# One encoder layer with attention and Hyena: folded taps in tiles of their own, part of the Hyena projection's splitting and stores on GpSimd, and the last attention unit's sums on VectorE

## The chip, the cores and the metric

The kernel runs on one NeuronCore of a Trainium2 chip. The metric is device time in microseconds (us), and lower is better. A core has five engines that each work through an instruction queue in order: TensorE (PE, with weight loads shown apart as PEld), VectorE (DVE), ScalarE (ACT), GpSimd (POOL) and SyncE (SP). In this kernel SP only issues DMA transfers; GpSimd and ScalarE can issue them too. Matmuls write to PSUM banks, and everything else lies in SBUF or HBM.

## What is computed

One layer of an encoder over 2048 tokens of width 1024, in float32. One projection gives queries, keys and values of a grouped-query attention (8 query heads, 2 key heads of 64) and the 1536 columns `u` of a Hyena operator:

```python
a = rms_norm(h, norm1_g[i])
proj = a @ w_in[i]
q, k, v, u = jnp.split(proj, [Q_WIDTH, Q_WIDTH + KV_WIDTH, Q_WIDTH + 2 * KV_WIDTH], axis=-1)
...
att = block_attention(q, k, v)
hy = hyena_mixer(u, hy_conv_w[i], hy_conv_b[i], filt_w1[i], ..., filt_deltas[i], hy_skip_d[i])
mix = jnp.concatenate([rms_norm(att, attn_out_g[i]), rms_norm(hy, hy_out_g[i])], axis=-1)
h = h + mix @ w_out[i]
m = rms_norm(h, norm2_g[i])
h = h + jnp.square(jax.nn.relu(m @ w_mlp_in[i])) @ w_mlp_out[i]
```

The Hyena operator first runs a convolution of width 3 over `u`. It then multiplies in the frequency domain by filters that a small network makes, with a decay, and divides them by the sum of their absolute values:

```python
h = h @ w4                                                   # hidden (2048 x 64) times w4 (64 x 2048)
h = h * jnp.exp(-t * jnp.abs(deltas)[None, :])
taps = jnp.concatenate([fwd, zeros, bwd[:0:-1]], axis=0)
taps = taps / jnp.sum(jnp.abs(taps), axis=0, keepdims=True)
return jnp.fft.rfft(taps, axis=0)
```

## The kernel before

**Precision.** A float32 product is made of three faster ones: each operand is split into a high part (a rounded copy, made by ScalarE) and a low part (the rest, made by VectorE), and TensorE adds high x low, low x high and high x high (L160 to L162).

**Stages.** (1) `qkv_proj` makes q, k and v, and runs the filter network's hidden layers beside it. Its order on each engine is the order of the code. (2) `attention`, from about 234 to 1193 us. (3) Transforms of the filters and the long convolutions, the mixing projection and the MLP, to the end at 3089.4 us. The change touches the end of the first stage and the second.

**u_proj** (L417 to L511) is a generator that the other stages pump, one step at a time. It makes `u` for four blocks of 512 tokens, and for each of them 12 column blocks of 128 columns; n counts both. In the first pass over the columns the weights are made as well. `load_raw` fetches a raw block of w_in (512 KB) on SP's queue. `split(n)` scales it into `uws`, eight slices each: ScalarE's high part (L448), VectorE's low part (L449), then one store of both parts to `uw_d` (1 MB, L452) for the later passes. Block n then takes 24 matmuls into the PSUM tile `uo`. ScalarE copies that to `u` (L497), which frees the bank, and makes the middle tap of the width-3 convolution, `uy` (L505). VectorE adds the two outer taps (L509), and a store on SP's queue writes `u_d` (256 KB, L511). While block n is multiplied, split(n + 1) runs. Two buffers (`uw12`) alternate, so split(n + 1) writes the buffer of block n - 1 and must wait until its matmuls are done and its store has landed. Raw blocks 1 and 2 are loaded ahead; for n from 1 to 9 the loop loads raw block n + 2 into one of two buffers (`ring`).

When `qkv_proj` has ended, 28 more steps of u_proj are pumped (START), which brings blocks up to n = 4 back to back; the rest runs beside attention.

**attention** (L541 on) has 32 units (2 key heads by 16 tiles of 128 tokens, 4 heads at once) of 16 steps. In this stage a scheduler sets the order of instructions on each engine. Some 22 steps ahead of its use, `peak` multiplies keys and queries (`sc`, L558) and VectorE takes the maximum (`top`, L561). `weights` multiplies again in higher precision (`st`, L578 and L579), ScalarE takes the exponential into a tile `p` (L581; a ring of PB = 14), and GpSimd adds the p of 16 steps: `sum` (L586), and at the last step its two halves into two tiles `os` (L591). `weighted` multiplies p by the values (`o`, L599); after a unit's last step ScalarE copies o's halves into `os` (L602), GpSimd adds both tiles (`ob`, L604), and `finish` turns the result with four matmuls (`of`, L610) and divides.

**Side work of attention.** Beside each step it pumps a mix: the first step of `taps_ahead`, 24 steps of u_proj, and then both in turns. `taps_ahead` (L1376 on) loads w4 in four pieces on GpSimd's queue (L1382), splits them (`w4h` on ScalarE, L1385, and w4l on VectorE), and makes 64 pieces of the taps of 128 channels by 512 positions. For each: an exponential of the decay on ScalarE (`ex`, L1403), two matmuls (`ft`, L1406), a product on VectorE (`taps`, L1408), the sum and the difference with the reversed taps on VectorE, written over `ex` (L1413, L1414), a store of these (`taps_d`, 256 KB, L1417, SP's queue), and on ScalarE the absolute values of the taps with their sum (L1418), written over `taps`. So a `taps` tile is read by both folds before L1418 may write it. `ex` tiles are a ring of three, `taps` tiles a ring of two; the w4 pieces lie in the same rings before.

Of the kernel before, what the change touches and what calls it, by code (L numbers as in the profile page):

```python
# [20 lines left out]
P = 128  # L21
# [16 lines left out]
def f32(ap):  # L38
    return ap.bitcast(F32)
# [386 lines left out]
def u_proj(k):  # L426
# [17 lines left out]
    def split(n, raw):  # L444

        w = uws[n and 2 - n % 2]
        for d in range(ND):
            nc.scalar.mul(out=w[:, 0, d], in_=raw[:, d], mul=k.g1[:, d:d + 1])  # L448
            nc.vector.scalar_tensor_tensor(out=w[:, 1, d], in0=raw[:, d], scalar=k.g1[:, d:d + 1],  # L449
                                           in1=f32(w[:, 0, d]), op0=ALU.mult, op1=ALU.subtract)  # L450
            yield
        nc.sync.dma_start(out=k.uw_d[n], in_=f32(w))  # L452
        yield
# [7 lines left out]
    uws += [pair[:, 0], pair[:, 1]]  # L461
    for n in (1, 2):
        raws[n] = load_raw(n, k.pa.tile([P, ND, P], F32, name="uraw", tag="xs", bufs=3)[:])
    yield
    for _ in split(1, raws[1]):
        yield
    k.up = sbuf(k, "up")
    pu = k.up.__enter__()
    edge = pu.tile([P, nct, 2], F32, name="edge", bufs=1)
    for n in range(NB * nct):  # L470
        b, ct = NB - 1 - n // nct, n % nct
        w = uws[n and 2 - n % 2]
        if n == 1:
            ring = k.uf.tile([P, 2, ND, P], F32, name="uraw", tag="U")
        if 0 < n < nct - 2:
            raws[n + 2] = load_raw(n + 2, ring[:, n % 2])
        parts = iter(())
# [30 lines left out]
        for tap in (0, 2):  # L508
            nc.vector.scalar_tensor_tensor(out=y[:, :m], in0=u[:, tap:tap + m], scalar=cw[:, tap, ct:ct + 1],  # L509
                                           in1=y[:, :m], op0=ALU.mult, op1=ALU.add)  # L510
        nc.sync.dma_start(out=k.u_d[ct * P:(ct + 1) * P, t0:t0 + m], in_=y[:, :m])  # L511

# [29 lines left out]
def attention(k, a1, ps, side):  # L542
# [6 lines left out]
    nc.vector.memset(fold[HD:, HD:], 1.0)  # L549
    one = a1.tile([P, P], F32, name="one", bufs=1)  # L550
    nc.vector.memset(one[:], 1.0)
    ones = a1.tile([P, P], F32R, name="ones", bufs=1)
    nc.vector.tensor_copy(out=ones[:], in_=one[:])

# [19 lines left out]
    def weights(u, j):  # L574
        s = ps.get("st", "st")
        b, c = j // 4, slice(j % 4 * P, (j % 4 + 1) * P)
        hi, lo = kt[u.kv, b]
        nc.tensor.matmul(s[:], lo[:, c], u.q2[:].rearrange("p h t -> p (h t)"), start=True, stop=False)  # L578
        nc.tensor.matmul(s[:], hi[:, c], u.q[:].rearrange("p h t -> p (h t)"), start=False, stop=True)  # L579
        p = a1.tile([P, 512], F32, name="p", bufs=PB)  # L580
        nc.scalar.activation(out=p[:], in_=s[:], func=AF.Exp)  # L581
        if j == 0:
            u.p0 = p
            u.sum = a1.tile([P, 512], F32, name="sum", bufs=2)
        elif j < 15:
            nc.gpsimd.tensor_add(out=u.sum[:], in0=u.p0[:] if j == 1 else u.sum[:], in1=p[:])  # L586
        else:
            u.os = [a1.tile([P, 512], F32, name="os", bufs=OSB) for i in range(2)]
            for i in range(2):
                rows = slice(i * HD, (i + 1) * HD)  # L590
                nc.gpsimd.tensor_add(out=u.os[i][HD:], in0=u.sum[rows], in1=p[rows])  # L591
        return u, j, p

    def weighted(u, j, p):
# [5 lines left out]
        if j == 15:  # L600
            for i in range(2):
                nc.scalar.copy(out=u.os[i][:HD], in_=u.o[i * HD:(i + 1) * HD])  # L602
            u.both = a1.tile([P, 512], F32, name="ob", bufs=1)
            nc.gpsimd.tensor_add(out=u.both[:], in0=u.os[0][:], in1=u.os[1][:])  # L604

# [62 lines left out]
SH = 2  # L668
PB = 14
RATE = 0.95  # L670
# [4 lines left out]
OSB = 2  # L675
UW_VEC = 0, 1, 2, 3, 4, 5, 6, 7

# [697 lines left out]
def filter_taps(k, f1, ps):  # L1375
    nc, a = k.nc, k.a  # L1376
    w4h = f1.tile([P, 4, HYW], F32R, name="w4h")
    w4l = f1.tile([P, 4, HYW], F32R, name="w4l")
    w4s = [f1.tile([P, HYW], F32, name="w4", tag=t, bufs=b) for t, b in (("ex", 3),) * 3 + (("taps", 2),)]
    for c, w4 in enumerate(w4s):  # L1380
# [12 lines left out]
    for b in range(4):  # L1393
        s = slice(b * 512, (b + 1) * 512)
        for i in range(2):
            tr = f1.tile([P, 512], F32, name="tr", bufs=2)
            nc.sync.dma_start(out=tr[:], in_=a["trow"][i:i + 1, s].to_broadcast([P, 512]))
            for o in range(2):
                for ct in range(4):
                    ci = o * 8 + i * 4 + ct  # L1400
                    cs = slice(ct * P, (ct + 1) * P)
                    ex = f1.tile([P, 512], F32, name="ex", bufs=3)
                    nc.scalar.activation(out=ex[:], in_=tr[:], func=AF.Exp, scale=dn[:, ci:ci + 1])  # L1403
# [5 lines left out]
                    if i == 1 and b == 0:  # L1409
                        nc.vector.memset(tp[:, 0:1], 0.0)  # L1410
                    x, e = (t[:].rearrange("p (s m) -> p s m", m=P) for t in (tp, ex))
                    back = x[:, :, ::-1][:, :, :HF]
                    nc.vector.tensor_add(out=e[:, :, :HF], in0=x[:, :, :HF], in1=back)  # L1413
                    nc.vector.tensor_sub(out=e[:, :, HF:], in0=x[:, :, :HF], in1=back)  # L1414
                    if i == 0 and b == 0:
                        nc.vector.tensor_copy(out=first[:, o, :, ct], in_=ex[:, 0:HF + 1:HF])
                    nc.sync.dma_start(out=k.taps_d[o, cs, i * SEQ + b * 512:i * SEQ + (b + 1) * 512], in_=ex[:])  # L1417
                    nc.scalar.activation(out=tp[:], in_=tp[:], func=AF.Abs,  # L1418
                                         accum_out=ab[:, o, ct, 4 * i + b:4 * i + b + 1])
# [447 lines left out]
def encoder_layer(tc, a):  # L1867
    with ExitStack() as ctx:
        k = setup(tc, ctx, a)
        with sbuf(k, "hid") as hid, sbuf(k, "early") as k.early:  # L1870
            k.hc = hid.tile([P, 2, SEQ], F32R, name="hc")
            with sbuf(k, "uf") as k.uf:
# [6 lines left out]
                with sbuf(k, "at") as at:  # L1879
                    with Banks(k, "ps2", {"st": 2, "sc": 3, "o": 1, "u": 2}) as k.ps:  # L1880
                        taps = taps_ahead(k, k.ps)
                        attention(k, at, k.ps, chain(islice(taps, 1), islice(k.u, UFIRST), mixed(taps, MA, k.u, MB)))
                k.up.__exit__(None, None, None)
        with sbuf(k, "wa") as k.wa:
# [36 lines left out]
```

## Time and profile before

| | us |
|---|---|
| median of 3 runs | 3090.89 |
| lowest, highest | 3089.37, 3095.59 |
| the profiled execution, its own time | 3091.2 |
| its span (first to last instruction) | 3089.4 |
| TensorE busy | 2968.5 (96%) |
| VectorE busy | 2082.4 (67%) |
| GpSimd busy | 1647.9 (53%) |
| ScalarE busy | 1388.5 (45%) |

The mean granted clock of TensorE is 0.985 of full speed. A row of a timeline has the start and the duration in us, then engine, line, operation, what is written and read, shape and count; in brackets stands the engine's idle time just ahead and what ended it. A row of a group has the count, the busy time in us and the mean of one in ns behind the shape. A row of the waits has the waiting engine, tile and line, what it waited for, the sum in us, how often, and the longest. A row of the chain has start and duration, then engine or DMA, tile and line. "SPq" is SP's queue; its durations there are those of the issue, not of the transfer. A row of windows gives for each engine the busy time and the count of instructions.

### The profile page before, as it was taken

How to read it: one execution, taken by the hardware profiler on the slowest of the kernel's cores; microseconds unless marked ns; L12 is line 12 of the kernel's file. 1: busy time of each engine (PE TensorE's matmuls, PEld its weight loads, DVE VectorE, ACT ScalarE, POOL GpSimd, SP SyncE). 2: the span in 40 equal slices, each digit the busy share in tenths (PEclk: the TensorE clock that was granted, in tenths of full speed). 3: DMA queues.
4: the chain of work that ended last, by engine and by line, in shares of the span. 5: the costliest groups of instructions: out<-in, count | busy, mean ns of one | idle time of the engine just before them, and what ended most of it. 6: DMA issues, size and time to landing. Idle time of an engine off the chain costs nothing.

```text
span 3089.4 us, 40268 instructions
## 1 busy us (share of the span) xinstructions
PE 2968.5 (96%) x13386; PEld 2237.0 (72%) x13386; DVE 2082.4 (67%) x3153; ACT 1388.5 (45%) x2593; POOL 1647.9 (53%) x1336
## 2 busy tenths in 40 slices
PE   7998999999999998999999889999999899999998
PEld 6785666666666666765758767887888688888887
DVE  6778887777777764667475568778877554454455
ACT  6765555555555545543435553334333233223333
POOL 4333787877778773015555128777877462250010
PEclk9998999999999999999999999999999999999999
DMA  8766433243342245875746875445544492433454
GB/s 248 217 192 208 143 115 108 95 156 104 104 150 102 96 131 170 287 254 189 215 137 198 288 266 164 154 150 204 181 157 153 152 355 99 142 108 130 150 184 150
DMA packets 452769, 525.74 MB, mean 170 GB/s; under 512 B 30443, under 2 KB 316769, under 8 KB 445521
## 3 DMA queue, kind: packets, MB, share of 16 engines
q1 hardware_dynamic: 442656, 502.44, 49.9%
q0 software_dynamic: 5856, 16.23, 1.6%
q10 hardware_dynamic: 4048, 4.49, 0.4%
q8 instruction: 107, 1.75, 0.2%
q14 instruction: 102, 0.83, 0.1%
HBM read 321.72 MB, written 193.99 MB: 167 GB/s over the span
## 4 chain that ended last, share of the span: by engine, by line
PE 78%; DVE 5%; issue 4%; POOL 3%; ACT 2%; DMA 2%; SPq 0%; ACTq 0%; POOLq 0%; DVEq 0%
PE o L599 7%; PE y L160 7%; PE y L161 7%; PE y L162 7%; PE g L161 6%; PE g L162 5%; PE g L160 5%; PE X L1543 4%; PE st L578 4%; PE sc L558 3%; PE st L579 3%; PE uo L162 2%; PE uo L161 2%; PE uo L160 2%; PE b L1678 2%
## 5 line engine op out<-in xcount | busy, mean ns | idle before, releaser
L586 POOL TENSOR_TENSOR sum<-sum,p 128x512 f32<-128x512 f32 x416 | 554.4, 1333 | 115.0 <-ACT p L581 89.6
L561 DVE TENSOR_REDUCE top<-sc 128x1 f32<-128x512 f32 x512 | 345.1, 685 | 172.4 <-PE sc L558 169.8
L581 ACT ACTIVATE p<-st 128x512 f32<-128x512 f32 x512 | 299.8, 596 | 227.5 <-PE st L579 215.5
L160 PE MATMUL g<-mh,wop 128*128 128x512 f32 x896 | 350.9, 392 | 6.8 <-ACT wop L1009 6.8
L161 PE MATMUL g<-ml,wop 128*128 128x512 f32 x896 | 351.0, 392 | 3.5 <-DVE ml L1020 3.5
L162 PE MATMUL g<-mh,wop 128*128 128x512 f32 x896 | 351.0, 392 | 1.9 <-DVE wop L1010 1.9
L160 PE MATMUL y<-bh,ah 128*128 128x512 f32 x768 | 299.7, 390 | 12.7 <-ACT ah L1214 12.7
L1193 DVE TENSOR_TENSOR ah<-ar,ah 128x1024 fp32r<-128x1024 f32 x111 | 150.0, 1352 | 223.9 <-ACT ah L1192 221.5
L161 PE MATMUL y<-bh,ah 128*128 128x512 f32 x768 | 299.5, 390 | 0.0
L162 PE MATMUL y<-bh,ah 128*128 128x512 f32 x768 | 299.4, 390 | 0.0
L1192 ACT CAST ah<-ar 128x1024 fp32r<-128x1024 f32 x111 | 117.0, 1054 | 337.9 <-PE y L162 329.7
L599 PE MATMUL o<-p,vt 128*64 128x512 f32 x1024 | 241.9, 604 | 0.0
L578 PE MATMUL st<-q,kt 128*128 128x512 f32 x512 | 213.9, 418 | 8.8 <-ACT p L581 8.6
L558 PE MATMUL sc<-kt,q 128*128 128x512 f32 x512 | 204.2, 402 | 16.9 <-DVE top L561 10.5
L579 PE MATMUL st<-q,kt 128*128 128x512 f32 x512 | 201.2, 393 | 0.0
L160 PEld LDWEIGHTS g<-mh,wop 128*128 128x128 f32 x896 | 169.6, 189 | 42.9 <-ACT wop L1009 7.5
L161 PEld LDWEIGHTS g<-ml,wop 128*128 128x128 f32 x896 | 169.3, 189 | 39.8 <-DVE ml L1020 4.5
L162 PEld LDWEIGHTS g<-mh,wop 128*128 128x128 f32 x896 | 169.3, 189 | 38.2 <-DVE wop L1010 3.1
L1009 ACT CAST wop<-ws 128x512 fp32r<-128x512 f32 x128 | 79.3, 621 | 229.1 <-PE g L162 177.4
L160 PEld LDWEIGHTS y<-bh,ah 128*128 128x128 f32 x768 | 144.7, 188 | 43.4 <-ACT ah L1214 13.1
L162 PEld LDWEIGHTS y<-bh,ah 128*128 128x128 f32 x768 | 144.5, 188 | 30.4 <-DVE ah L1215 0.3
L599 PEld LDWEIGHTS o<-p,vt 128*64 128x64 f32 x1024 | 68.6, 137 | 134.7 <-issue 134.7
(331 smaller groups left out, 7027.0 us busy)
## 6 DMA issues: line engine op xcount, KB each, us to landing
ar<-H_d SPq DMA_DIRECT2D x109, 512.0 KB, 3.8
uw<-uw_d SPq DMA_DIRECT2D x36, 1024.0 KB, 4.9
w1raw<-in_w_mlp_in SPq DMA_DIRECT2D x64, 512.0 KB, 4.1
H_d<-r SPq DMA_DIRECT2D x96, 256.0 KB, 2.2
H_d<-s SPq DMA_DIRECT2D x96, 256.0 KB, 2.0
F_d<-F SPq DMA_DIRECT2D x34, 512.0 KB, 3.3
F<-F_d SPq DMA_DIRECT2D x34, 512.0 KB, 3.8
taps_d<-ex SPq DMA_DIRECT2D x64, 256.0 KB, 2.0
```

The lines of the kernel that those rows point to most:

```text
L160: mm(out, l_hi, r_hi, start=start, stop=False)
L161: mm(out, l_hi, r_lo, start=False, stop=False)
L162: return mm(out, l_lo, r_hi, start=False, stop=stop)
L558: nc.tensor.matmul(s[:], u.q[:, h], kt[u.kv, b][0][:], start=True, stop=True)
L561: nc.vector.tensor_reduce(out=u.top[:, h, b:b + 1], in_=s[:], axis=AX.X, op=ALU.max, negate=True)
L578: nc.tensor.matmul(s[:], lo[:, c], u.q2[:].rearrange("p h t -> p (h t)"), start=True, stop=False)
L579: nc.tensor.matmul(s[:], hi[:, c], u.q[:].rearrange("p h t -> p (h t)"), start=False, stop=True)
L581: nc.scalar.activation(out=p[:], in_=s[:], func=AF.Exp)
L586: nc.gpsimd.tensor_add(out=u.sum[:], in0=u.p0[:] if j == 1 else u.sum[:], in1=p[:])
L599: nc.tensor.matmul(u.o[cols], vt[j // 8][:, j % 8, u.kv], p[:], start=j < 2, stop=j > 13)
L1193: nc.vector.tensor_sub(out=h[:, 1], in0=raw[:], in1=f32(h[:, 0]))
L1543: k.nc.tensor.matmul(d[:, ri], t[:, m], Af[:, 2 * j + at], start=True, stop=True)
```

## The change

1. **Taps.** The folds write a new tile `both` (a ring of two), which the store reads. L1418 writes the absolute values over `ex`, no longer over `taps`. `ex` becomes a ring of two; the four w4 pieces lie two in `ex`'s slots and two in `taps`'s.
2. **Low parts.** In split(2) to split(8) every second slice's low part is made by GpSimd, as a product into `uwg` (one buffer) and a difference: 28 pairs of instructions of 128 x 128 in place of 28 on VectorE.
3. **Stores.** For n below 9 (UPOOL) the stores of `uw_d` and of `u_d` are issued on GpSimd's queue.
4. **Raw blocks.** Block 3 is loaded ahead together with 1 and 2; blocks 4 and 5 both at n = 1; from n = 4 on as before.
5. **Last unit.** The adds of `sum`, `os` and `ob` of the last of the 32 units run on VectorE (`u.adder`).
6. PB goes from 14 to 13, and a tile of ones is made from `ident` in one step without its helper tile. `k.up` becomes the pool's tile source, `k.up_pool` the pool.

```diff
@@ u_proj: split
-            nc.vector.scalar_tensor_tensor(out=w[:, 1, d], in0=raw[:, d], scalar=k.g1[:, d:d + 1],
-                                           in1=f32(w[:, 0, d]), op0=ALU.mult, op1=ALU.subtract)
+            if 1 < n < UPOOL and d % 2:
+                t = k.up.tile([P, P], F32, name="uwg", bufs=1)
+                nc.gpsimd.tensor_mul(out=t[:], in0=raw[:, d], in1=k.g1[:, d:d + 1].to_broadcast([P, P]))
+                nc.gpsimd.tensor_sub(out=w[:, 1, d], in0=t[:], in1=f32(w[:, 0, d]))
+            else:
+                nc.vector.scalar_tensor_tensor(out=w[:, 1, d], in0=raw[:, d], scalar=k.g1[:, d:d + 1],
+                                               in1=f32(w[:, 0, d]), op0=ALU.mult, op1=ALU.subtract)
             yield
-        nc.sync.dma_start(out=k.uw_d[n], in_=f32(w))
+        (nc.gpsimd if n < UPOOL else nc.sync).dma_start(out=k.uw_d[n], in_=f32(w))
@@ u_proj: loads and the store of u
-    for n in (1, 2):
+    for n in (1, 2, 3):
         raws[n] = load_raw(n, k.pa.tile([P, ND, P], F32, name="uraw", tag="xs", bufs=3)[:])
-        if 0 < n < nct - 2:
-            raws[n + 2] = load_raw(n + 2, ring[:, n % 2])
+        for i in (4, 5) if n == 1 else (n + 2,) if 3 < n < nct - 2 else ():
+            raws[i] = load_raw(i, ring[:, i % 2])
-        nc.sync.dma_start(out=k.u_d[ct * P:(ct + 1) * P, t0:t0 + m], in_=y[:, :m])
+        (nc.gpsimd if n < UPOOL else nc.sync).dma_start(out=k.u_d[ct * P:(ct + 1) * P, t0:t0 + m], in_=y[:, :m])
@@ attention
-            nc.gpsimd.tensor_add(out=u.sum[:], in0=u.p0[:] if j == 1 else u.sum[:], in1=p[:])
+            u.adder.tensor_add(out=u.sum[:], in0=u.p0[:] if j == 1 else u.sum[:], in1=p[:])
-                nc.gpsimd.tensor_add(out=u.os[i][HD:], in0=u.sum[rows], in1=p[rows])
+                u.adder.tensor_add(out=u.os[i][HD:], in0=u.sum[rows], in1=p[rows])
-            nc.gpsimd.tensor_add(out=u.both[:], in0=u.os[0][:], in1=u.os[1][:])
+            u.adder.tensor_add(out=u.both[:], in0=u.os[0][:], in1=u.os[1][:])
+        u.adder = nc.vector if n == NKV * NT - 1 else nc.gpsimd
-PB = 14
+PB = 13
+UPOOL = 9
@@ taps_ahead
-    w4s = [f1.tile([P, HYW], F32, name="w4", tag=t, bufs=b) for t, b in (("ex", 3),) * 3 + (("taps", 2),)]
+    w4s = [f1.tile([P, HYW], F32, name="w4", tag=t, bufs=b) for t, b in (("ex", 2), ("taps", 2)) * 2]
-                    ex = f1.tile([P, 512], F32, name="ex", bufs=3)
+                    ex = f1.tile([P, 512], F32, name="ex", bufs=2)
-                    x, e = (t[:].rearrange("p (s m) -> p s m", m=P) for t in (tp, ex))
+                    both = f1.tile([P, 512], F32, name="both", bufs=2)
+                    x, e = (t[:].rearrange("p (s m) -> p s m", m=P) for t in (tp, both))
-                    nc.sync.dma_start(out=k.taps_d[o, cs, i * SEQ + b * 512:i * SEQ + (b + 1) * 512], in_=ex[:])
-                    nc.scalar.activation(out=tp[:], in_=tp[:], func=AF.Abs,
+                    nc.sync.dma_start(out=k.taps_d[o, cs, i * SEQ + b * 512:i * SEQ + (b + 1) * 512], in_=both[:])
+                    nc.scalar.activation(out=ex[:], in_=tp[:], func=AF.Abs,
```

How the change moves instructions is shown at three places. ScalarE at the start of attention: `uw` is the high part of column block 5, `w4h` the split of w4, `u` and `uy` the end of column block 4. In the old kernel (copy at L497):

```order
L448 ACTIVATE uw_2253<-uraw,g_110 128x128 x8
L1385 CAST w4h<-w_2879 128x512
L1385 CAST w4h<-w_2880 128x512
L1385 CAST w4h<-w_2881 128x512
L497 COPY u<-uo 128x512
L505 ACTIVATE uy<-u,cb,cw 128x511
```

In the new kernel (the copy is L502 there, the tap's exponential L1407):

```order
L448 ACTIVATE uw_2253<-uraw,g_110 128x128 x8
L1389 CAST w4h<-w_2909 128x512
L1389 CAST w4h<-w_2910 128x512
L1407 ACT_TABLE_LOAD
L1407 ACTIVATE ex<-tr,dn 128x512
L502 COPY u<-uo 128x512
L1389 CAST w4h<-w_2911 128x512
L510 ACTIVATE uy<-u,cb,cw 128x511
```

Two casts stand ahead of the copy in place of three, and a table load and the first tap's exponential moved ahead of it.

GpSimd at the same place, from the last work of `qkv_proj` to the first sums of attention. In the old kernel only the eight loads of w4 stand between:

```order
L316 CAST kk<-unit 128x2x64
L1382 DMA w_2878<-in_filt_w 64x512 x2
L1382 DMA w_2879<-in_filt_w 64x512 x2
L1382 DMA w_2880<-in_filt_w 64x512 x2
L1382 DMA w_2881<-in_filt_w 64x512 x2
L586 TENSOR_TENSOR sum<-p 128x512
```

In the new kernel a part of what stands there: the last of block 3's low parts (L451 and L452, product and difference), its store (L457) and the store of u of block 2 (L516); the store of u of block 1 and three more of block 3's pairs stand right ahead:

```order
L451 TENSOR_TENSOR uwg<-uraw,g_110 128x128
L452 TENSOR_TENSOR uw_2253<-uwg,uw_2253 128x128
L1386 DMA w_2909<-in_filt_w 64x512
L457 DMA uw_d<-uw_2253 128x2048
L516 DMA u_d<-uy 128x511
L451 TENSOR_TENSOR uwg<-uraw,g_110 128x128
L1386 DMA w_2909<-in_filt_w 64x512
L452 TENSOR_TENSOR uw_2253<-uwg,uw_2253 128x128
L1386 DMA w_2910<-in_filt_w 64x512
```

Low parts, both kinds of stores and the loads of w4 now share one queue, in this order.

VectorE at the end of attention, where `r` and `ao` belong to the unit before the last and `uy` to u_proj; the old kernel has none of the L589, L594 and L607 rows on VectorE. The new kernel:

```order
L589 TENSOR_TENSOR sum<-p 128x512
L589 TENSOR_TENSOR sum<-sum,p 128x512 x2
L514 SCALAR_TENSOR_TENSOR uy<-u,cw,uy 128x513
L589 TENSOR_TENSOR sum<-sum,p 128x512
L615 RECIPROCAL r<-of 128x4
L589 TENSOR_TENSOR sum<-sum,p 128x512
L617 TENSOR_TENSOR ao<-of,r 128x256
L514 SCALAR_TENSOR_TENSOR uy<-u,cw,uy 128x513
L589 TENSOR_TENSOR sum<-sum,p 128x512 x9
L594 TENSOR_TENSOR os<-sum,p 64x512 x2
L607 TENSOR_TENSOR ob<-os 128x512
```

All sixteen of the last unit's sums, and `ob`, are now in VectorE's queue, behind that work.

More of the change, by code (lines that the diff above doesn't have):

```diff
@@ L466, in u_proj @@
         yield
-    k.up = sbuf(k, "up")
-    pu = k.up.__enter__()
+    k.up_pool = sbuf(k, "up")
+    pu = k.up = k.up_pool.__enter__()
     edge = pu.tile([P, nct, 2], F32, name="edge", bufs=1)
@@ L549, in attention @@
     nc.vector.memset(fold[HD:, HD:], 1.0)
-    one = a1.tile([P, P], F32, name="one", bufs=1)
-    nc.vector.memset(one[:], 1.0)
     ones = a1.tile([P, P], F32R, name="ones", bufs=1)
-    nc.vector.tensor_copy(out=ones[:], in_=one[:])
+    nc.vector.tensor_scalar(out=ones[:], in0=k.ident[:], scalar1=0.0, scalar2=1.0, op0=ALU.mult, op1=ALU.add)
     def peak(u, i):
@@ L675 @@
 OSB = 2
-UW_VEC = 0, 1, 2, 3, 4, 5, 6, 7
+UPOOL = 9
 NOP = 8
@@ L1415, in filter_taps @@
                     if i == 0 and b == 0:
-                        nc.vector.tensor_copy(out=first[:, o, :, ct], in_=ex[:, 0:HF + 1:HF])
-                    nc.sync.dma_start(out=k.taps_d[o, cs, i * SEQ + b * 512:i * SEQ + (b + 1) * 512], in_=ex[:])
-                    nc.scalar.activation(out=tp[:], in_=tp[:], func=AF.Abs,
+                        nc.vector.tensor_copy(out=first[:, o, :, ct], in_=both[:, 0:HF + 1:HF])
+                    nc.sync.dma_start(out=k.taps_d[o, cs, i * SEQ + b * 512:i * SEQ + (b + 1) * 512], in_=both[:])
+                    nc.scalar.activation(out=ex[:], in_=tp[:], func=AF.Abs,
                                          accum_out=ab[:, o, ct, 4 * i + b:4 * i + b + 1])
@@ L1882, in encoder_layer @@
                         attention(k, at, k.ps, chain(islice(taps, 1), islice(k.u, UFIRST), mixed(taps, MA, k.u, MB)))
-                k.up.__exit__(None, None, None)
+                k.up_pool.__exit__(None, None, None)
         with sbuf(k, "wa") as k.wa:
```

## The prediction

> **What bounds the kernel now.** I read the page's chain of waits first, then the windows around the two ends of the attention stage, where the change works, then the timelines of the engines there. The chain:
>
> ```profile
> PE 78%; DVE 5%; issue 4%; POOL 3%; ACT 2%; DMA 2%; SPq 0%; ACTq 0%; POOLq 0%; DVEq 0%
> ```
>
> TensorE carries 78% of the path, and nothing here removes a matmul. So the change can only win where TensorE waits or is granted a slow clock. The windows (columns: us; busy time of PE, PEld, DVE, ACT, POOL; granted clock; DMA share; GB/s) show where:
>
> ```profile
> 234.00:240.00 6.00, 0.53 (x3) 0.29 (x2) 4.00 (x13) 4.78 (x13) 0.00 (x0) 0.90 1.03 374
> 240.00:246.00 6.00, 6.00 (x16) 4.64 (x16) 5.61 (x12) 2.95 (x9) 0.00 (x0) 0.53 1.01 326
> 272.00:276.00 4.00, 4.00 (x8) 1.43 (x8) 4.00 (x7) 2.66 (x5) 3.76 (x4) 0.62 0.20 70
> 280.00:300.00 20.00, 15.70 (x55) 8.65 (x53) 18.68 (x32) 8.23 (x17) 11.54 (x8) 0.84 0.40 125
> 1186.00:1192.00 6.00, 0.34 (x2) 0.22 (x2) 0.00 (x0) 1.16 (x2) 5.44 (x5) 0.93 0.04 11
> 1192.00:1198.00 6.00, 6.00 (x29) 6.00 (x30) 1.29 (x3) 1.23 (x3) 0.00 (x0) 0.50 0.22 67
> ```
>
> Three places: a stop at the start of attention (234 to 240), a stretch where VectorE is full and TensorE is not (280 to 300), and a stop at the end (1186 to 1192). A stop is paid twice: the 6 us behind each long one run at a clock of 0.53 or 0.50. The stops themselves, with what ended them:
>
> ```profile
> 239.71 1.22 PE L558 MATMUL sc<-kt,q 128*128 128x512 f32 x2 [5.47 <-ACT u L497]
> 271.97 0.50 PE L558 MATMUL sc<-kt,q 128*128 128x512 f32 x1 [2.21 <-DVE top L561]
> 1191.78 1.97 PE L610 MATMUL of<-fold,ob 128*128 128x65 f32 x8 [5.66 <-POOL ob L604]
> ```
>
> So an idle of 5.5 us cost about 3 us more in clock (6 x 0.5), and one of 2.21 us cost 1.5 (4 x 0.38).
>
> **Part 1, the last unit's sums on VectorE (tail).** GpSimd's and ScalarE's work on the last unit:
>
> ```profile
> 1169.58 18.17 POOL L586 TENSOR_TENSOR sum<-sum,p 128x512 f32<-128x512 f32 x13
> 1187.82 2.57 POOL L591 TENSOR_TENSOR os<-sum,p 64x512 f32<-64x512 f32 x2
> 1183.04 1.09 ACT L581 ACTIVATE p<-st 128x512 f32<-128x512 f32 x2 [1.05 <-PE st L579]
> 1186.81 0.58 ACT L602 COPY os<-o 64x512 f32<-64x512 f32 x1
> ```
>
> The last weights p are there at 1184.13, but GpSimd adds at 1.40 us each and ends its row of sums only at 1187.75. The only VectorE instruction of this size with both inputs in SBUF that stands beside idle GpSimd is this one, 0.68 us:
>
> ```profile
> L566 DVE TENSOR_TENSOR diag<-ident,low 128x512 fp32r<-128x512 f32 x1 | 0.7, 682 | 0.0
> ```
>
> I cost each add on VectorE at 0.68. Weights come about 1.07 apart (two in 1.09 plus a wait of 1.05), so VectorE keeps up: last sum at about 1184.3, the two os adds by 1185.7, before ScalarE's copies end at 1187.39. Then ob takes 0.7 and `of` starts near 1188.15: 3.6 earlier. The idle is 5.66 - 3.6 = 2.0, close to the 2.21 of the second row above, so I let the clock lose 1.5 and not 3.0: 1.5 more. Sum **-5.1**; ends -3.6 (clock as before) and -6.6 (no slow clock at all). A rule of the Trainium skill bears on the clock: "TensorE: Matmul & The Clock Gate", section "What's actually happening", has the throttle come after an idle window of about 3.4 us. The row at 271.97, where 2.21 us was followed by 0.62, speaks against it here; by the rule the tail would give 1.5 more and the total 3079.0.
>
> **Part 2, folded taps in tiles of their own (steady state).** Absolute values (L1418) overwrite the taps, so ScalarE waits for VectorE's folds; and the next exponential (L1403), whose tile ring the folds and their stores share, waits for a store of a folded tap:
>
> ```profile
> ACT taps L1418 <- DVE ex L1414: 107.5, 54, 5.0
> PE st L578 <- ACT p L581: 7.5, 9, 1.9
> 645.89 0.50 PE L578 MATMUL st<-q,kt 128*128 128x512 f32 x1 [1.92 <-ACT p L581]
> 913.82 0.50 PE L578 MATMUL st<-q,kt 128*128 128x512 f32 x1 [1.55 <-ACT p L581]
> 1058.13 0.50 PE L578 MATMUL st<-q,kt 128*128 128x512 f32 x1 [1.87 <-ACT p L581]
> 644.15 0.63 ACT L1418 ACTIVATE taps<-taps 128x512 f32<-128x512 f32 x1 [1.80 <-DVE ex L1414]
> 911.36 0.72 ACT L1403 ACTIVATE ex<-tr,dn 128x512 f32<-128x512 f32 x1 [1.86 <-DMA taps_d<-ex]
> 1055.67 0.72 ACT L1403 ACTIVATE ex<-tr,dn 128x512 f32<-128x512 f32 x1 [1.31 <-DMA taps_d<-ex]
> ```
>
> ScalarE's 107.5 us of waiting is not on the path; TensorE's 7.5 us behind it is (330 to 1150). Three stops make 1.92 + 1.55 + 1.87 = 5.3 of it, each right behind one of these ScalarE waits. In the new code both waits go: Abs needs only the product, and no store reads an `ex` tile any more. ScalarE still waits for the product behind VectorE's queue; I keep 0.8 for that and take **-4.5**; ends 0 (every stop comes back under another name) and -7.5 (all nine go). What the fold now waits for, the store of `both` two taps ago, stands on VectorE, with the reductions queued behind it; that store's landing lies a whole tap back, so nothing. One p buffer fewer: 0, at most the 3 us of the two shorter stops.
>
> **Part 3, the first column blocks (head).** The chain at the start is one ScalarE queue: the block's high parts (L448) wait, behind them the w4h casts, behind them the copy of u (L497) that frees the PSUM bank for `sc`:
>
> ```profile
> 223.30 0.89 SPq L452 DMA_DIRECT2D uw_d<-uw  x1
> 224.24 10.84 DMA uraw<-in_w_in
> 235.19 2.44 ACT L448 ACTIVATE uw<-uraw,g 128x128 fp32r<-128x128 f32 x8 [3.33 <-DMA uraw<-in_w_in]
> 237.54 1.64 ACT L1385 CAST w4h<-w 128x512 fp32r<-128x512 f32 x3
> 239.09 0.57 ACT L497 COPY u<-uo 128x512 f32<-128x512 f32 x1
> 253.87 1.28 ACT L1403 ACT_TABLE_LOAD   x1
> 255.16 0.72 ACT L1403 ACTIVATE ex<-tr,dn 128x512 f32<-128x512 f32 x1
> ```
>
> Raw block 5 now leaves two blocks of u_proj sooner, so that wait goes. What is late next: the high parts of block 5 go into the buffer of block 3, whose store (uw_d) must have landed. That store moves to GpSimd's queue, behind the store of u of block 1, which can't leave before it did on SP, and behind block 3's eight low-part instructions and a load of w4. Prices:
>
> ```profile
> 220.45 1.49 SPq L511 DMA_DIRECT2D u_d<-uy  x1
> L282 POOL TENSOR_TENSOR y<-y,qkg 128x128 f32<-128x128 f32 x16 | 7.4, 464 | 11.9 <-ACT y L280 11.8
> L1382 POOL DMA_DIRECT2D w<-in_filt_w x8 | 4.2, 559 | 3.7 <-issue 3.7
> DMA to landing us min/median/max: 10.4/10.4/10.4
> uw_d<-uw SPq DMA_DIRECT2D x12, 1024.0 KB, 5.0
> ```
>
> 220.45 + 0.56 + 8 x 0.464 + 0.56 = 225.3 for its issue. Landing takes 5.0 (the median of all twelve) to 10.4 (this store before, with the DMA engines at a share of 1.03). I take some 9, near the crowded one, because the stretch stays crowded: 234. Behind it on ScalarE now stand 2.44 of high parts, two casts of w4h (1.1), the table load and one exponential (1.28 + 0.72, moved ahead of the copy), then the copy 0.57: 6.1, so `sc` starts at about 240.2 against 239.71: **+0.5**, and the half clock stays. Ends: landing in 5.0 gives 230.3 + 6.1 = 236.4, 3.2 earlier, and a shorter idle saves 1.3 of clock (2.8 less 1.5): -4.5; landing in 10.4 gives +2.2, and I allow +4 for the store of u before it being late.
>
> **Part 4, half the low parts on GpSimd (VectorE's full stretch).** Blocks 2 to 5 lie ahead of attention, where the wait above decides. Blocks 6 to 8 lie in 246 to 320, where VectorE ends TensorE's waits:
>
> ```profile
> L449 DVE SCALAR_TENSOR_TENSOR uw<-uraw,g,uw 128x128 fp32r<-128x128 f32 x55 | 18.9, 387 | 4.6 <-ACT uw L448 4.6
> L449 DVE SCALAR_TENSOR_TENSOR uw<-uraw,g,uw 128x128 fp32r<-128x128 f32 x33 | 23.8, 738 | 0.2 <-ACT uw L448 0.2
> L561 DVE TENSOR_REDUCE top<-sc 128x1 f32<-128x512 f32 x53 | 35.6, 680 | 10.8 <-PE sc L558 10.7
> ```
>
> The first row is of 190 to 262, with GpSimd nearly idle, the others of 262 to 362, with its sums running: one low part costs VectorE 387 ns alone and 738 beside GpSimd. Twelve fewer: 8 x 0.387 + 4 x 0.738 = 6.0. But 24 new GpSimd instructions lie beside VectorE's other work there and can stretch it as its sums did, and two w4 low parts move behind the start (2 x 0.68 = 1.4). I take **-1.5**; ends -8 (nothing stretched, a slow-clock gap gone as well) and +5.
>
> **Sum.** The profiled run took 3091.2 (span 3089.4): 3091.2 - 5.1 - 4.5 + 0.5 - 1.5 = 3080.6. The median of the three runs is 0.3 lower: **3080.5**. A measurement of this kernel tells about 0.2% (6.2 us) from no change: faster is below 3084.7, slower above 3097.1. Part 1's direction is sure, part 3's is not.
>
> **The rivals.**
>
> *The head stop shrinks.* The store lands in 5.0, since the raw loads before it went earlier: -4.5 instead of +0.5, 3075.5. For it: L452's median. Against it: the 10.84 and 1.03 above. The Trainium skill ("DMA: Bandwidth & Descriptors", section "Anatomy of one DMA — SWDGE (gpsimd) path") has about 2.0 us plus bytes over 436 GB/s, an estimate of 4.4 us for this store; no run here shows a store of 1 MB from that queue.
>
> *GpSimd and VectorE hold each other up.* If the 28 low parts of these blocks that stay on VectorE, and some 16 folds and adds beside them, pay 738 - 387 = 351 ns each, that is 44 x 0.351 = +15.4, against 28 removed at 387: -10.8. Net +4.6 in place of -1.5: 3086.6, no change that can be told. For it: the two L449 rows. Against it: L561 reads PSUM and kept 680, and half of those low parts lie where VectorE isn't what ends the waits. The Trainium skill ("SBUF — State Buffer", section "Who interferes with whom") has VectorE with two SBUF inputs and a GpSimd read exclude each other; the L449 rows agree.
>
> *Slower: GpSimd's issue becomes the bound of the head.* If GpSimd pays for a store by its bytes, 0.559 for 128 KB makes 4.5 for uw_d and 1.1 for u_d; with 3.7 of low parts a block costs GpSimd 9.3 us. TensorE needs 5.5 for one:
>
> ```profile
> 214.91 0.23 PE uo L162
> ```
>
> (24 matmuls x 0.23). Blocks 2 to 5 stand back to back: 4 x 3.8 = 15.2 later, and two more idles of the 2.21 kind, 3.0 of clock: 3080.5 - 0.5 + 18.2 = 3098.2. It decides once a uw_d issue holds GpSimd for over 0.7 us (5.5 - 3.7 - 1.1). Against it: a transfer of twice the bytes costs no more there:
>
> ```profile
> L887 POOL DMA_DIRECT2D mo_d<-sb x20 | 10.7, 540 | 37.4 <-DVE sb L890 37.0 <-issue 0.4
> ```
>
> (256 KB each.)
>
> *The tail doesn't come.* VectorE's adds are queued behind the last uy and ao work and end no sooner than GpSimd's: 3080.5 + 5.1 = 3085.6, no change that can be told. Against it: VectorE did nothing at all in 1186 to 1192.
>
> **How the numbers follow.** Forecast 0.45 (own range 3077 to 3086, from parts 2 and 4 at half their ends), head stop shrinks 0.22, mutual hold-up 0.16, slower head 0.09, no tail 0.08. Faster: most of the first two cases, some of the third: 0.64; same 0.27; slower 0.09. The range takes the lucky head with part 4 at its good end (3075.5 - 4.5 = 3071) and, above, the hold-up case with part 2 gone (3086.6 + 4.5 = 3091, and a little): 3071 to 3092.
>
> **What would show it.** Right: in the new profile the idle ahead of `of` is about 2 us and ended by VectorE; ScalarE's wait ahead of Abs is for the product and far below 107.5; the stop ahead of the first `sc` is still 5 us or so, and the high parts ahead of it wait for the store of uw_d, not a raw block; L449's group in 262 to 362 has some 12 fewer. Wrong: a first `sc` before 237; GpSimd holding a uw_d issue for several us; new stops of TensorE ended by GpSimd between blocks 2 and 5; VectorE's low parts at 738 ahead of 262.

## The result and the profile after

| | us | ratio to before, 95% interval |
|---|---|---|
| before, 5 runs | 3089.37 (3084.97 to 3095.59) | |
| changed, 5 runs | 3071.11 (3067.70 to 3076.92) | 0.9941 (0.9924 to 0.9959) |
| changed again (e12), 5 runs beside another 11 of before | 3075.80 (3071.14 to 3080.44) | 0.9957 (0.9944 to 0.9969) |

The kernel became faster by 18 us in the first set and 13 in the second (0.43% of 3088); the forecast was 10.4. Both medians lie below the likeliest case's own range (3077 to 3086), and the first, 3071.11, only just inside the whole range (3071 to 3092). The profiled execution of the changed kernel took 3076.92, the slowest of its five; its span is 3075.1, 14.3 less than before. Where these 14.3 come from is read at four marks of both traces:

| mark | before, us | after, us | difference |
|---|---|---|---|
| first copy of u behind `qkv_proj`'s blocks (block 0) | 213.01 | 213.44 | +0.4 |
| copy of u of block 5 | 250.07 | 261.82 | +11.8 |
| 33rd exponential p | 330.36 | 333.28 | +2.9 |
| last exponential p | 1183.53 | 1174.20 | -9.3 |
| last `of` | 1191.78 | 1178.90 | -12.9 |
| end of the span | 3089.4 | 3075.1 | -14.3 |

So the head lost 11, the stretch in which VectorE is full gave 9 of them back, the steady part gained 12, and the tail 3.6 and a little clock.

**Head.** Windows of the changed kernel (columns as before the change: us; PE, PEld, DVE, ACT, POOL; clock; DMA share; GB/s):

```profile
238.00:244.00 6.00, 1.20 (x2) 0.50 (x2) 1.55 (x4) 2.50 (x9) 2.63 (x6) 0.77 1.04 287
244.00:250.00 6.00, 2.49 (x7) 1.99 (x7) 4.25 (x9) 5.19 (x8) 4.29 (x9) 0.50 1.05 345
272.00:276.00 4.00, 4.00 (x19) 3.15 (x18) 3.97 (x7) 3.40 (x9) 3.63 (x7) 1.00 0.75 259
280.00:300.00 20.00, 16.69 (x71) 10.68 (x70) 20.00 (x31) 11.91 (x25) 16.69 (x15) 1.00 0.37 132
```

Its stops of TensorE, ScalarE's waits ahead of them, and the landing of the two stores that those wait for (issued on GpSimd at 222.36 and 228.99, in this order):

```profile
231.51 0.50 PE L160 MATMUL uo<-A,uw 128*128 128x512 f32 x1 [2.11 <-ACT uw L448]
242.80 0.79 PE L162 MATMUL uo<-A,uw 128*128 128x512 f32 x1 [4.96 <-POOL uw L452]
247.53 1.22 PE L561 MATMUL sc<-kt,q 128*128 128x512 f32 x2 [3.51 <-ACT u L502]
```

```profile
231.06 2.45 ACT L448 ACTIVATE uw<-uraw,g 128x128 fp32r<-128x128 f32 x8 [6.22 <-DMA uw_d<-uw]
241.50 2.45 ACT L448 ACTIVATE uw<-uraw,g 128x128 fp32r<-128x128 f32 x8 [6.67 <-DMA uw_d<-uw]
```

```profile
DMA to landing us min/median/max: 8.6/8.6/8.6
DMA to landing us min/median/max: 12.4/12.4/12.4
```

There are now two blocks (4 and 5) whose high parts wait for a store, and the `sc` that waits for the copy of u stands at 247.53, 7.8 later than before. (One `sc` stands ahead of it in both kernels; the prediction calls the waiting one the first.) The stop of 4.96 ends with GpSimd's last low part of block 4. That one stood in GpSimd's queue behind a load of w4 which, by the profile, waited for the same store:

```profile
241.71 0.55 POOL L1386 DMA_DIRECT2D w<-in_filt_w  x1 [3.04 <-DMA uw_d<-uw]
```

It doesn't set the time of the waiting `sc`, though: the copy of u that this `sc` needs stands on ScalarE behind the high parts of 241.50. Behind the stops the clock is 0.77 and 0.50. In 272 to 300 the clock is 1.00, where it was 0.62 and 0.84, and TensorE does 71 matmuls in 280 to 300 instead of 55; in 300 to 320, with the head 12 us late, it is 0.91 and 69 matmuls, where it was 0.99 and 74.

**Steady part.** The waits of the changed kernel from 330 to 1150, and behind them two rows of before that the prediction does not show:

```profile
PEld st L581 <- ACT p L584: 8.0, 25, 0.7
PE st L581 <- ACT p L584: 0.5, 2, 0.3
ACT ex L1423 <- DVE taps L1412: 10.3, 12, 2.0
ACT ex L1423 <- DVE taps L1414: 3.2, 6, 1.3
```

```profile
PEld st L578 <- ACT p L581: 19.3, 35, 2.4
ACT ex L1403 <- DMA taps_d<-ex: 32.1, 36, 1.9
```

ScalarE's 107.5 us of waiting for folds became 10.3 for products and 3.2 for VectorE's zeroing of a first tap (L1414), its 32 us for stores are gone, and TensorE's stops behind p went from 7.5 to 0.5. Its weight loads waited 19.3 us for p before and 8.0 now.

**Tail.** VectorE's last adds and TensorE's stop:

```profile
1175.17 1.39 DVE L594 TENSOR_TENSOR os<-sum,p 64x512 f32<-64x512 f32 x2
1178.15 0.69 DVE L607 TENSOR_TENSOR ob<-os 128x512 f32<-128x512 f32 x1 [1.60 <-ACT os L605]
```

```profile
1178.90 1.11 PE L613 MATMUL of<-fold,ob 128*128 128x65 f32 x8 [2.05 <-DVE ob L607]
```

The adds take 0.69 each, `ob` waits for ScalarE's copies and no longer for sums, and the stop is 2.05 instead of 5.66.

### The profile page after: what moved, and what is told of

Read it like the earlier page. It is cut to its first block, busy times and chain, and to the rows that moved or that the text cites. A ratio compares the mean times of both kernels' runs of the same rounds, so it can differ in the third digit from the quotient of the medians.

```text
span 3075.1 us, 40358 instructions
## 1 busy us (share of the span) xinstructions
PE 2959.2 (96%) x13386; PEld 2236.4 (73%) x13386; DVE 2078.5 (68%) x3141; ACT 1390.6 (45%) x2593; POOL 1664.9 (54%) x1393
## 4 chain that ended last, share of the span: by engine, by line
PE 51%; issue 3%; POOL 2%; DMA 2%; DVE 2%; ACT 1%; ACTq 0%; SPq 0%; POOLq 0%; DVEq 0%
PE y L160 7%; PE y L161 7%; PE y L162 7%; PE g L162 5%; PE g L161 5%; PE g L160 5%; PE X L1548 4%; PE fs L1574 2%; PE b L1683 2%; PE yo L1748 2%; PE cs L1650 1%; PE op L162 1%; PE op L160 1%; PE op L161 1%; DMA ml<-sb 1%
## 5 line engine op out<-in xcount | busy, mean ns | idle before, releaser
L589 POOL TENSOR_TENSOR sum<-sum,p 128x512 f32<-128x512 f32 x403 | 536.8, 1332 | 103.4 <-ACT p L584 78.5
L160 PEld LDWEIGHTS y<-bh,ah 128*128 128x128 f32 x768 | 144.5, 188 | 43.0 <-ACT ah L1218 13.1
L162 PEld LDWEIGHTS y<-bh,ah 128*128 128x128 f32 x768 | 144.5, 188 | 30.4 <-DVE ah L1219 0.3
L161 PEld LDWEIGHTS y<-bh,ah 128*128 128x128 f32 x768 | 144.5, 188 | 30.0
```

The source lines that it names most:

```text
L160: mm(out, l_hi, r_hi, start=start, stop=False)
L161: mm(out, l_hi, r_lo, start=False, stop=False)
L162: return mm(out, l_lo, r_hi, start=False, stop=stop)
L589: u.adder.tensor_add(out=u.sum[:], in0=u.p0[:] if j == 1 else u.sum[:], in1=p[:])
```

## The experiments

From these traces came theory A: the parts add up, the tail gives 5, the tiles of their own 12, and the head costs 3. The rival B had the gain along attention come from the new head. Ratios are to the runs of before on the same chip.

| run | what stands in it | median us | ratio, interval |
|---|---|---|---|
| e1 | before + tail | 3081.77 | 0.9976 (0.9966 to 0.9986) |
| e2 | before + tiles, PB 13 | 3073.94 | 0.9952 (0.9939 to 0.9965) |
| e3 | before + tail + tiles | 3064.76 | 0.9927 (0.9914 to 0.9940) |
| e4 | before + new head | 3094.04 | 1.0017 (1.0008 to 1.0025) |
| e5 | changed, stores back on SP | 3063.17 | 0.9909 (0.9896 to 0.9923) |
| e6 | changed, low parts back on VectorE | 3078.61 | 0.9957 (0.9944 to 0.9971) |
| e7 | changed, raw blocks as before | 3074.99 | 0.9948 (0.9935 to 0.9960) |
| e8 | e3 + early raw blocks | 3065.90 | 0.9919 (0.9905 to 0.9932) |
| e9 | changed, only u_d back on SP | 3071.86 | 0.9944 (0.9932 to 0.9957) |
| e10 | changed, only uw_d back on SP | 3069.47 | 0.9939 (0.9925 to 0.9952) |
| e11 | e3, absolute values over taps | 3080.18 | 0.9973 (0.9962 to 0.9984) |
| e12 | changed | 3075.80 | 0.9957 (0.9944 to 0.9969) |

**e1, the tail alone.**

```diff
+        u.adder = nc.vector if n == NKV * NT - 1 else nc.gpsimd
-            nc.gpsimd.tensor_add(out=u.sum[:], ...
+            u.adder.tensor_add(out=u.sum[:], ...
```

(Not shown: the same for `os` and `ob`.)

> The kernel before with one edit alone: the last unit's sum, os and ob adds on VectorE. Theory A (the parts add up: tail -4.8, taps -12, head +3): 3089.4 - 4.8 = about 3084.6, and the idle ahead of the last `of` is about 2.05 us and ended by VectorE. Rival B (the gain along attention comes from the new head, the tiles of their own give only the three stops, -4.5): the same for this run.

0.24% faster, 7.4 us of 3089 (4 to 10). Its stop in the timeline:

```profile
1188.47 1.10 PE L610 MATMUL of<-fold,ob 128*128 128x65 f32 x8 [2.04 <-DVE ob L604]
```

**e2, the tiles alone.**

```diff
+                    both = f1.tile([P, 512], F32, name="both", bufs=2)
-                    nc.scalar.activation(out=tp[:], in_=tp[:], func=AF.Abs,
+                    nc.scalar.activation(out=ex[:], in_=tp[:], func=AF.Abs,
-PB = 14
+PB = 13
```

(Not shown: `both` in the folds and the store, the rings of `ex` and of the w4 pieces, and the tile of ones, as in the change.)

> The kernel before with the folded taps in tiles of their own and PB = 13 alone. Theory A: about -12, so 3077; TensorE's idle between the 33rd and the last exponential falls from 12.4 to some 4 us. Rival B: -4.5, so 3085; idle there falls to some 7 us.

0.48%, 14.8 us (11 to 19). In its trace the way from the 33rd to the last exponential takes 841.7 us, before 853.2: 11.4 less, on the old head. TensorE's idle time on this way falls from 12.4 to 4.0, as theory A had it. The other 3.1 are busy time of about as many matmuls (840.8 before, 837.7 here): a matmul's row lasts some 0.39 where the starts are 0.23 apart (before, 231.81 and 232.04), so a short stop can lie hidden in busy time. Rival B falls. PB = 13 is a part of this edit and was not tested alone.

**e3, both.** The edits of e1 and e2 together.

> Tail and tiles together on the old head, so the changed kernel without everything in the first column blocks (low parts, stores, raw blocks). Theory A: -4.8 - 12 = about 3072.5, and as the head costs 3 in the profile, at or a little below the changed kernel's 3071 to 3074. Rival B: -9.3, so 3080, clearly above the changed kernel.

0.73%, the sum of e1 and e2 (0.72), and no slower than the changed kernel; the median of 3064.76 is below what either theory expected. So all that stands in the first column blocks together gives nothing.

**e4, the head alone.** The edits of e1 and e2 taken out of the changed kernel, PB left at 13.

> The changed kernel without the tail and without the tiles of their own (PB stays 13): the new first column blocks alone. Theory A: +3 (the 33rd exponential 2.9 later in the profile, nothing after it), so 3092; the copy of u of block 5 some 12 us later than before. Rival B: -9 or so, 3080. A third possibility is that the head varies from run to run, and its median is below the old one by the 4 us that the profiled run of the changed kernel lies above its median: 3088.

0.17% slower, 5.3 us (2.5 to 7.7), as theory A had it. Its profiled execution, 3087.17, was the lowest of its 12. It shows the copy of block 5 6.3 late, not 12, and the 33rd exponential 2.8 sooner than before (block 0 was 1.6 sooner already), so the loss itself is told by the times, not by that trace.

**e5 to e8, which part of the head.** Stores, low parts and raw blocks were taken back one at a time; e8 leaves the raw blocks alone.

```diff
e5
-        (nc.gpsimd if n < UPOOL else nc.sync).dma_start(out=k.uw_d[n], in_=f32(w))
+        nc.sync.dma_start(out=k.uw_d[n], in_=f32(w))
-        (nc.gpsimd if n < UPOOL else nc.sync).dma_start(out=k.u_d[ct * P:(ct + 1) * P, t0:t0 + m], in_=y[:, :m])
+        nc.sync.dma_start(out=k.u_d[ct * P:(ct + 1) * P, t0:t0 + m], in_=y[:, :m])
e6
-            if 1 < n < UPOOL and d % 2:
+            if False:
e7
-    for n in (1, 2, 3):
+    for n in (1, 2):
-        for i in (4, 5) if n == 1 else (n + 2,) if 3 < n < nct - 2 else ():
-            raws[i] = load_raw(i, ring[:, i % 2])
+        if 0 < n < nct - 2:
+            raws[n + 2] = load_raw(n + 2, ring[:, n % 2])
```

(e8 has the edits of e5 and e6.)

> The changed kernel with the stores of uw_d and u_d back on SP's queue; low parts stay half on GpSimd, raw blocks early, tail and tiles as changed. Theory S (the head's loss is the stores: on GpSimd's queue they leave behind its low parts, SP runs ahead with nine loads, and ScalarE's high parts wait 6 to 7 us for each store to land): the loss goes, 0.9927 of before or better, about 3065 or a little below. Rival G (the loss is GpSimd's low parts, two instructions each and one after the other): stays at about 0.9941, 3071.

> The changed kernel with all low parts back on VectorE; stores stay on GpSimd's queue. Theory S: the stores leave some 4 us sooner, since no low parts stand ahead of them on that queue, so a part of the loss goes, but VectorE gets 28 low parts back in its full stretch: 3069 to 3073. Rival G: the whole loss goes, 3065.

> The changed kernel with the raw blocks loaded as before. Theory S: ScalarE then waits for stores and raw blocks alike, no better than the changed kernel: 3071 to 3076. A rival R (the early raw loads crowd the stores out): 3066.

> Tail, tiles and the early raw blocks; stores on SP and all low parts on VectorE. Theory S: raw block 5 no longer ends the wait ahead of the first `sc`, the store of uw_d of block 3 does, at 233.7 as before, 1.4 sooner than the raw block: 1 to 3 us better than without (3062 to 3064). Rival R: the loads meet the stores and it is no better or worse, 3065 to 3068.

e5 has the lowest median and ratio of all (its interval overlaps those of e8 and e3): moving the stores to GpSimd cost 0.32 points against the first set of the changed kernel and 0.48 against e12, 10 to 15 us. Rival G falls, since e6 is no faster; at 3078.61 it is slower than theory S expected, too (3069 to 3073). The low parts on GpSimd are a small gain by the medians (e5 against e8 0.10 points, the changed kernel's first set against e6 0.16, e12 against e6 none), but the intervals overlap each time. Early raw blocks come to 0.08 points (e8 against e3), which the intervals don't tell from none, and its 3065.90 lies where rival R had it; e7 is within the changed kernel's two sets. The traces put the low parts' gain where VectorE is full: from the copy of block 5 to the 33rd exponential the distance to before shrinks by 11.4 us in e5 (-1.9 to -13.3) and by 3.3 in e8 (-4.0 to -7.3); by 8.8 in the changed kernel (11.2 in e12) and by 3.2 in e6. The low parts that stay on VectorE, in e8 and then in e5, first from 190 to 262 and then from 262 to 362:

```profile
L454 DVE SCALAR_TENSOR_TENSOR uw<-uraw,g,uw 128x128 fp32r<-128x128 f32 x56 | 19.0, 384 | 3.9 <-ACT uw L448 3.9
L454 DVE SCALAR_TENSOR_TENSOR uw<-uraw,g,uw 128x128 fp32r<-128x128 f32 x32 | 15.5, 522 | 3.7 <-ACT uw L448 3.7
```

```profile
L454 DVE SCALAR_TENSOR_TENSOR uw<-uraw,g,uw 128x128 fp32r<-128x128 f32 x32 | 22.9, 734 | 0.1
```

```profile
L454 DVE SCALAR_TENSOR_TENSOR uw<-uraw,g,uw 128x128 fp32r<-128x128 f32 x28 | 19.6, 717 | 0.5 <-ACT uw L448 0.5
```

From 262 on, beside GpSimd's sums, GpSimd's low parts did not make VectorE's dearer in this pair (734 and 717 ns). Ahead of 262 they did: 522 ns instead of 384, which takes back 4.4 us of VectorE's time (32 x 0.138) of the 9.2 that the 24 moved ones saved there (24 x 0.384).

What the stores do is seen on SP's queue. The changed kernel:

```profile
220.94 4.49 SPq L524 DMA_DIRECT2D kt<-k_d  x4
225.47 1.25 SPq L543 DMA_DIRECT2D vt<-v_d  x1
226.84 0.88 SPq L1401 DMA_DIRECT2D tr<-in_trow  x1
227.76 2.45 SPq L524 DMA_DIRECT2D kt<-k_d  x2
230.25 1.54 SPq L1401 DMA_DIRECT2D tr<-in_trow  x1
231.84 4.70 SPq L524 DMA_DIRECT2D kt<-k_d  x4
238.70 22.17 SPq L441 DMA_DIRECT2D uraw<-in_w_in  x3
```

and e5:

```profile
222.47 0.74 SPq L524 DMA_DIRECT2D kt<-k_d  x1
224.57 0.32 SPq L516 DMA_DIRECT2D u_d<-uy  x1
224.94 2.22 SPq L524 DMA_DIRECT2D kt<-k_d  x3
227.21 1.44 SPq L543 DMA_DIRECT2D vt<-v_d  x1
228.75 3.61 SPq L441 DMA_DIRECT2D uraw<-in_w_in  x1
232.47 4.45 SPq L457 DMA_DIRECT2D uw_d<-uw  x1
237.01 0.50 SPq L516 DMA_DIRECT2D u_d<-uy  x1
237.99 0.88 SPq L457 DMA_DIRECT2D uw_d<-uw  x1
242.36 0.32 SPq L516 DMA_DIRECT2D u_d<-uy  x1
242.74 0.45 SPq L441 DMA_DIRECT2D uraw<-in_w_in  x1
243.27 0.66 SPq L1401 DMA_DIRECT2D tr<-in_trow  x1
```

Without stores in its way SP issues thirteen loads for attention and the taps from 220.94 to 236.5, and raw block 6 comes behind them. In e5 five of them are out by 228.65, raw block 6 follows, and the stores hold the others back. The DMA engines are full either way (their share from 232 to 242 is 1.05 before, 1.01 in the changed kernel and 1.08 in e5); what differs is which transfers stand in front.

**e9 and e10, which of the two stores.** The diff of e5, each with one of its two halves.

> The changed kernel with only the stores of u_d back on SP; those of uw_d stay on GpSimd's queue. Theory U (what costs is uw_d: the next split's high parts wait for its landing): the loss stays, 3071 to 3076. Rival D (what costs is u_d, which waits for VectorE at the head of GpSimd's queue and holds low parts and uw_d behind it): the loss goes, 3061 to 3065.

> The mirror: only the stores of uw_d back on SP; u_d stays on GpSimd's queue. Theory U: the loss goes, 3061 to 3065. Rival D: it stays, 3071 to 3076.

Both keep the loss (0.9944 and 0.9939 against e5's 0.9909), so neither theory U nor rival D holds. ScalarE in e9:

```profile
243.54 1.28 ACT L1407 ACT_TABLE_LOAD   x1 [4.97 <-DMA tr<-in_trow]
244.84 0.72 ACT L1407 ACTIVATE ex<-tr,dn 128x512 f32<-128x512 f32 x1
245.46 0.57 ACT L502 COPY u<-uo 128x512 f32<-128x512 f32 x1
```

Here no high part waits long for a store (1.45 us at most up to block 5), and the `sc` behind the copy of u is still at 246.08, after an idle of 13.23: the table load and the first tap's exponential stand ahead of the copy of u and wait 4.97 for `tr`, a load that landed 14.8 us after its issue (in e10 the same wait is 4.71). In e5 that exponential stands behind the copies of blocks 4 and 5 too, the same `sc` starts at 237.92, and no wait for `tr` is left. So in e9 and e10 two things happen: SP's loads run ahead into full DMA engines, and the program puts the tap's exponential ahead of the copy. The trace of e6 shows that the second is not needed for the late `sc`. There the table load stands behind that copy (at 252.32) and no high part waits more than 0.95 for a store, and still the `sc` comes only at 249.09, after an idle of 14.96. The program put one high part of block 6 ahead of the copy, and that one waits for its raw block, issued on SP at 230.46:

```profile
248.16 0.40 ACT L448 ACTIVATE uw<-uraw,g 128x128 fp32r<-128x128 f32 x1 [13.21 <-DMA uraw<-in_w_in]
```

In all fourteen traces the waiting `sc` sorts by the queue of the stores. With all of them on SP (before, e1, e2, e3, e5, e8, e11) it starts 25.4 to 27.1 us behind the copy of u of block 0, with some or all of them on GpSimd (changed, e4, e6, e7, e9, e10, e12) 33.2 to 38.6. In each of the late ones ScalarE stands in front of that copy for a transfer that lands late, but not for the same one: the store of `uw_d` (changed, e4, e12), `tr` (e7, e9, e10) or a raw block (e6). The order on ScalarE is the scheduler's, and it differs among these kernels. How much of the 10 us comes from the late landings and how much from an order that puts a waiting instruction in front, these runs don't separate.

**e11, which of ScalarE's two waits.**

```diff
-                    nc.scalar.activation(out=ex[:], in_=tp[:], func=AF.Abs,
+                    nc.scalar.activation(out=tp[:], in_=tp[:], func=AF.Abs,
```

> The old head with the tail and the folds in tiles of their own, but the absolute values written over the taps tile again, so that ScalarE waits for VectorE's folds as before, while its exponential no longer waits for a store. Theory F (the 11 us between the 33rd and the last exponential come from ScalarE no longer waiting for the folds): 8 to 11 of them are lost, 3073 to 3076. Rival W (they come from the exponential no longer waiting for a store, as two of the three stops of the prediction): 2 or 3 are lost, 3066 to 3068.

It lost 0.46 points against e3, 14 us (7 to 22 by the ends of both intervals). That is far from rival W's 2 or 3 and more than theory F's 8 to 11; its 3080.18 lies above theory F's range, too. In the traces 7.8 of the 16.1 us between the spans of e11 and e3 lie ahead of the last `of`, and the rest behind it, where the two kernels don't differ. Its waits from 330 to 1150:

```profile
ACT taps L1418 <- DVE both L1414: 80.4, 55, 2.5
PEld st L576 <- ACT p L579: 15.5, 32, 2.4
PE st L576 <- ACT p L579: 5.2, 7, 1.9
```

The way from the 33rd to the last exponential is 849.3 us: 853.2 before, 849.3 here, 842.1 in e3. The weight loads' waits for p are 19.3, 15.5 and 7.9. The steps are 3.8 and 7.6 of waiting, 3.8 and 7.2 of time. So of these 11 us about 7 come from no longer waiting for the folds and about 4 from no longer waiting for a store, one trace each.

**e12, the changed kernel again.**

> The changed kernel once more, beside the others on the same chip: 0.994 of before as it was, 3071 to 3074 where before is 3089 to 3092; its copy of u of block 5 is again some 12 us late in the profile.

The median of 3075.80 lies above the 3071 to 3074 that were expected, and the gain is 13 us, not 18. The copy of block 5 is 7.0 late this time, not 12, and the 33rd exponential is 4.2 sooner than before (block 0 was 1.9 sooner already). One profile of this head is good to about 5 us.

## Why the prediction was right, and where its steps were not

The direction and the likeliest case's reason for it (tail and steady part) held. That the time fell into the range is in part luck: the range's low end stood for a head stop that shrinks, the head's stops grew instead, and the time got there because the steady part gave far more than was priced. The total came near through errors of opposite signs.

- **Part 1, tail, -5.1: right.** From the last exponential to `of` it is 8.25 us before and 4.70 after, 3.55 less for a forecast of 3.6; adds of 0.69 for 0.68, an idle of 2.05 for 2.0. The clock gave 1.3 in this trace (0.72 over the next 6 us) and 3.0 in most others (below). e1 has 7.4 (4 to 10).
- **Part 2, steady part, -4.5: the right mechanism, mis-sized by a factor of 2.5 to 3.** It measured -12.3 in the trace and 14.8 in e2's times, outside the term's own end of -7.5. The step that failed took TensorE's 7.5 us of stops behind p for all that lies on the path, from the row of the matmuls alone. Weight loads run ahead of their matmuls (the one for the `sc` at 643.57 in the trace of before starts 0.23 sooner) and wait for the same p. Their row of 19.3 us fell by 11.3, close to the 11.4 of e2's way. It is no second cost beside the matmuls' row: the stop at 645.89 stands in both, with 1.92 for the matmul and 2.36 for its weight load. That every microsecond of that row costs one of time is not shown; that the two move together is, in the three traces of e11's paragraph. Also, two of the three stops were put on the wait for a store; by e11's trace that wait made 3.8 of the 11 us, and the wait for the folds the rest.
- **Part 3, head, +0.5: right in the resource, wrong in its size and incomplete.** That the high parts of block 5 wait for the store of block 3 is what the trace shows. But its issue came at 228.99 and not 225.3, since the store of u of block 1 left at 223.14 and not 220.45 (block 2's low parts and store stand ahead of it on GpSimd), it took 12.4 and not 9, and block 4 had the same wait, 6.22, for the store of block 2. The step priced the queue that the stores join and put nothing for the queue that they leave: what SP does without them. The waiting `sc`: +7.8 instead of +0.5, or +6.1 in e12.
- **Part 4, VectorE's full stretch, -1.5: right in sign, too small.** -8.8 (with stretches that the late head merely pushed there), or about 8 by e5 against e8 in single traces, the term's good end; the times give 0 to 5. Contention was allowed for; in e5 it came ahead of 262 (522 ns for e8's 384, above) and not behind it.
- **The sum:** parts 3 and 4 together were put at -1.0 and measured +2.5 (first trace) and -2.3 (e12) between the marks of block 0 and the 33rd exponential; by the times the new head costs 5.3 (e4).
- **The signs.** Of the signs of being right, the idle of 2.05 ended by VectorE, ScalarE's short wait for the product and the wait of the high parts for `uw_d` came; the stop ahead of the waiting `sc` is 3.51, with the one of 4.96 a little ahead of it. That 262 to 362 would hold some 12 low parts fewer on VectorE did not: 32 in the changed kernel and 28 in e5, for 33 before. By part 4's own sum (8 x 0.387 + 4 x 0.738) only four of the twelve lay there, and the late head pushed four others in. Of the signs of being wrong one came: the stop of 4.96 ended by GpSimd, for the reason told above and not for the price of an issue.
- **Rivals.** The head stop did not shrink. The mutual hold-up came in part, in e5 at 138 ns for a low part instead of 351, and did not outweigh what was moved. GpSimd's issue is not paid by bytes, as the rows of the changed kernel show, 1 MB and 256 KB:

```profile
L457 POOL DMA_DIRECT2D uw_d<-uw x9 | 5.2, 577 | 3.2 <-DVE u L492 1.2 <-POOL uw L452 1.0 <-DVE uw L454 0.9
L516 POOL DMA_DIRECT2D u_d<-uy x9 | 5.1, 572 | 12.8 <-DVE uy L514 8.6 <-DMA k_d<-qs 2.3 <-DVE u L492 1.7
```

The slower head came all the same, with late landings and not by the length of an issue.

The gain in short: the tail and the folds in tiles of their own make 0.73%; the low parts make 6 to 8 us by the traces (5.6, 8.0 and 8.1 in three pairs) and 0 to 5 by the times, which do not settle it; the stores on GpSimd's queue take 10 or more back. With the stores on SP (e5) the kernel is 0.91% faster than before, 29 us by the medians, and faster than the changed kernel; whether it is also faster than e3, without any of the new head, the intervals don't tell.

## What to carry to other kernels

A wait in front of TensorE can stand in two rows, its matmuls' and its weight loads'. They overlap, so don't add them, but read both before you price what another engine's stall costs: here the matmuls' row was too small (7.5 us, for a gain of 11 to 12) and the weight loads' nearer. When a transfer is moved to another queue, price the queue that it leaves as well: what stood behind it there starts sooner, and where the DMA engines are full, as here, another transfer may land later for it. Test a bundle's parts one at a time even when the bundle is faster, since one part can hide a loss as large as the others' gain.

## What the runs showed of the hardware that was not expected

- **The clock behind a short idle.** Eleven of the profiled executions have a TensorE idle of 2.04 or 2.05 us ahead of the last `of`. In the next 6 us the granted clock was 1.00 in eight of them and 0.72 in three (the changed kernel, e5, e11); behind 5.66 or 5.67 us it was 0.50 to 0.53 each time (before, e2, e4). The rule of the Trainium skill that the prediction weighed ("TensorE: Matmul & The Clock Gate", section "What's actually happening", an idle window of about 3.4 us) fits the eight and not the three.
- **Stores of one size land in very different times.** In the changed kernel a 1 MB store took 4.2 us on GpSimd's queue at 206 (the DMA share while it was under way was 0.78), 8.6 at 222 and 12.4 at 229 (1.01 both times), while loads of `kt` issued on SP around 236 took up to 17.6.
- **The same kernel's span varies outside the change.** From TensorE's stop ahead of `n` to the one ahead of the first `g` (1532.12 to 1830.43 before) it is 298.3 us before and 294.3 to 303.9 in four executions whose edits lie all ahead of it (e1 to e4), so one profile can't tell a change of 5 us by its span.
